# Cross attention in a one-core encoder layer: two heads' values in one 512-column projection, the attention's small products put at stated steps of the projections, and the last two heads' products moved later

## The chip, the cores and the metric

The kernel runs on one core of a Trainium2 chip. The metric is device time in microseconds (us), the median of several runs; lower is better. The profile shows one execution of the same program.

## The reference

One encoder layer (256 tokens, width 2048, float32) has four sub-layers: a feed-forward block, a pair of gated token mixers, a cross attention to 256 memory tokens, and a second feed-forward block. Each reads a normalized x and adds a normalized output to x. The change is in the cross attention, where four heads of width 256 attend from 256 tokens to 256 memory tokens:

```python
D_MODEL, SEQ, N_MEM, MEM_HEADS, MEM_HEAD = 2048, 256, 256, 4, 256

def memory_xattn(h, mem, n_mem, w_cq, w_ckv, w_co):
    B, S, _ = h.shape
    M = mem.shape[1]
    q = (h @ w_cq).reshape(B, S, MEM_HEADS, MEM_HEAD)
    kv = (rmsnorm(mem, n_mem) @ w_ckv).reshape(B, M, MEM_HEADS, 2 * MEM_HEAD)
    k, v = kv[..., :MEM_HEAD], kv[..., MEM_HEAD:]
    s = jnp.einsum('bqhd,bmhd->bhqm', q, k).astype(jnp.float32) * (MEM_HEAD ** -0.5)
    p = jax.nn.softmax(s, axis=-1).astype(v.dtype)
    o = jnp.einsum('bhqm,bmhd->bqhd', p, v).reshape(B, S, MEM_HEADS * MEM_HEAD)
    return o @ w_co

# in the layer, after the mixers:
h = rmsnorm(x, n_x_pre[l])
x = x + rmsnorm(memory_xattn(h, mem, n_mem[l], w_cq[l], w_ckv[l], w_co[l]), n_x_post[l])
```

## The kernel before

**Projections.** A float32 weight matrix streams from HBM in tiles of 128 x 1024 numbers (`wraw`, four buffers, loaded by the SP queue). ACT writes the rounded part of a tile to `whi` (line 368) and DVE the remainder to `wlo` (line 369); both are rings of three slots, so the split of a tile waits until TensorE (PE) has done with the tile three before it. Activations are kept as two such parts too (`hT`, `mT`, `oT`). PE then makes three products where a plain one would make one.

There are two forms of a projection. `lin_ch` leaves the result with channels on partitions: the weights are stationary, and per step k (128 rows of the weight) and per 128 channels there is one product with both parts of the activations as 512 moving columns (line 424) and one of `wlo` with 256 columns (line 428). `lin_tok` leaves tokens on partitions: the activations are stationary, the weights move, and per step k and per 128 tokens t there are three products as wide as the projection's column block (lines 463, 464, 465). Both are generators that yield at steps: `lin_ch` once per k, `lin_tok` once per (k, t). The result is in PSUM: `psm` (tag `mm`, four banks) for projections, `pst` (tag `tr`, two) and `pss` (tag `sm`, two) for small products.

**The cross attention** (`xattn`). `kv(h)` makes one head's keys (`lin_ch`, 256 columns, tile `kT`) and values (`lin_tok`, 256 columns, tile `xv`, copied out of PSUM by ACT at line 1829). `query(h)` is a `lin_ch` of 256 columns. `attend(h, q)` makes, for each half t of the tokens, the scores (line 1854, tile `xsc`), their softmax (maximum on DVE, lines 986 and 987; exponential on ACT, line 989; division on DVE, lines 990 and 991; tile `p`), and the two 128 x 128 transposes of `p` (line 1859, tile `xpt`), which ACT copies to `pT` (line 1860); then the values' products (line 1865, tile `xo`) and their split into `oT` (line 656, ACT and DVE). Scores and values are plain float32, which PE takes in two passes each.

**What sets the order.** The keys and values of heads 0 and 1 come first, then those of head 2 beside the normalization of x (`pre_norm`: 32 transposes of x, tile `tr`, line 691, split into `hT` at lines 658 and 659), then the queries and the heads, then head 3's keys and values, then the output projection `w_co` (`lin_tok`, four blocks of 512 columns) with head 3's attention inside its first block. Where the program says nothing, a list scheduler orders each engine's instructions by priority (the order in which they are written) and by its own estimate of when operands are ready; on each engine the resulting order is fixed, and an engine waits at an instruction whose operands are late. Inside `tc.manual_schedule(engines={PE})` PE's instructions keep the order in which they are written. The weights of `w_ckv` are laid out on the host in blocks (`_CUTS`), one block after another in the order of the loads.

Of the kernel before, what the change touches and what calls it, by code (L numbers as in the profile page):

```python
# [10 lines left out]
F32 = mybir.dt.float32  # L11
F32R = mybir.dt.float32r
I32 = mybir.dt.int32
AF = mybir.ActivationFunctionType
# [4 lines left out]
P = 128  # L19
D = 2048  # L20
T = 256
NT = T // P
KD = D // P
# [205 lines left out]
class Layer:  # L229
# [396 lines left out]
    def row(self, r):  # L626

        nc = self.nc
        ps = self.pss.tile([P, T], F32, tag="sm", name="rB")
        for t in range(NT):  # L630
            nc.tensor.matmul(
                ps[:, t * P : (t + 1) * P], r[t].broadcast_to([P, P]), self.ident, start=True, stop=True)
# [1180 lines left out]
    def xattn(self, m, xsp):  # L1813
        nc, a, tc = self.nc, self.a, self.tc
        with tc.tile_pool(name="xat", bufs=1) as pool:
            squares = pool.tile([P, 2, 8, T], F32, tag="oT", name="squares")
            squares = [squares[:, i] for i in range(2)]
            mem, feed = self.pre_norm_input(a["memT"], "n_mem", pool, squares)
            mr, mrow = self.square_stats(squares)
            todo = [lambda k=k: feed(k, 4) for k in range(0, KD, 4)] + [mr, int, mrow]  # L1820
            update = self.mix_out(*m, xsp, lambda: todo and todo.pop(0)())
            kT = pool.tile([P, 8, T], F32, name="kT")
            v = pool.tile([P, NT, 1024], F32, name="xv")

            def kv(h):
                self.lin_ch(a["w_ckv"], KD, h * 512, 256, mem,
                            lambda j, ps: nc.vector.tensor_mul(kT[:, 2 * h + j, :], ps, mrow()))
                self.lin_tok(a["w_ckv"], KD, h * 512 + 256, 256, mem[:, :, 0], mem[:, :, 1],
                             lambda t, ps: nc.scalar.activation(
                                 out=v[:, t, h * 256 : (h + 1) * 256], in_=ps, func=AF.Copy, scale=mr()[t]))  # L1830
# [12 lines left out]
            def query(h):  # L1843
                q = pool.tile([P, 2, T], F32, tag="q", name="q", bufs=4)
                self.lin_ch(a["w_cq"], KD, h * 256, 256, hq,
                            lambda j, ps: nc.vector.tensor_mul(q[:, j, :], ps, row()))
                return q

            def attend(h, q):
                pT = pool.tile([P, 2, T], F32, tag="pT", name="pT", bufs=2)  # L1850
                for t in range(NT):
                    ps = self.pss.tile([P, T], F32, tag="sm", name="xsc")
                    for j in range(2):
                        nc.tensor.matmul(  # L1854
                            ps, q[:, j, t * P : (t + 1) * P], kT[:, 2 * h + j, :], start=(j == 0), stop=(j == 1))
                    p = self.softmax(pool, ps, 1.0 / 16)
                    pt = self.pst.tile([P, 2, P], F32, tag="tr", name="xpt")
                    for j in range(2):
                        nc.tensor.transpose(pt[:, j, :], p[:, j * P : (j + 1) * P], self.ident)
                    nc.scalar.copy(out=pT[:, :, t * P : (t + 1) * P], in_=pt)  # L1860
                for j in range(2):
                    po = self.pss.tile([P, T], F32, tag="sm", name="xo")
                    for m in range(NT):
                        vs = slice(h * 256 + j * P, h * 256 + (j + 1) * P)
                        nc.tensor.matmul(po, v[:, m, vs], pT[:, m, :], start=(m == 0), stop=(m == NT - 1))  # L1865
# [10 lines left out]
            return self.post_norm(  # L1876
                lambda c, ev, passage: self.lin_tok(
                    a["w_co"], 8, c * 512, 512, o[:, 0], o[:, 1], ev, 8 * (c == 3), passage),
                a["n_x_post"], False, "n_ffn2_pre", None, xsp)

    def store(self, update):
        for t in range(NT):
# [7 lines left out]
def layer(ctx: ExitStack, tc, a):  # L1890
# [21 lines left out]
_MOVING = {"w_ukv": lambda i, m: False, "w_ckv": lambda i, m: i % 2 == 1}  # L1912
_ROWS = ("n_ffn1_post", "n_mix_post", "n_x_post", "n_ffn2_post", "b_gate", "lnx_w", "lnx_b")


def _tiles(w, cuts, moving):

    nk, out, c0 = w.shape[0] // P, [], 0
    if isinstance(cuts, int):
        cuts = [cuts] * (w.shape[1] // cuts) + [w.shape[1] % cuts] * (w.shape[1] % cuts > 0)  # L1920
    for i, n in enumerate(cuts):
        kt = WT // n
        order = np.arange(n).reshape(-1, 2).T.reshape(-1) if moving(i, n) else np.arange(n)
        for k in range(0, nk, kt):
            out.append(w[k * P : (k + kt) * P, c0 + order].reshape(-1, P, n).transpose(1, 0, 2).reshape(-1))
        c0 += n
    assert c0 == w.shape[1]
    return np.concatenate(out)


def _wide_tiles(w):

    out, order = [], np.arange(512).reshape(-1, 2).T.reshape(-1)
    ks = [k for item in _wide_order() for k in (item if isinstance(item, tuple) else (item,))]
    for c0 in range(0, D, WT):
        for k in ks:
            out.append(w[k * P : (k + 1) * P, c0 + np.concatenate([order, 512 + order])].reshape(-1))
        for h in range(2):
            for k in range(WIDE, KF, 2):
                x = w[k * P : (k + 2) * P, c0 + h * 512 + order]  # L1940
                out.append(x.reshape(-1, P, 512).transpose(1, 0, 2).reshape(-1))
    return np.concatenate(out)


def _layout(inputs):
    f = lambda n: np.ascontiguousarray(np.asarray(inputs[n]))
    arr = {"x": f("x")[0], "mem": f("mem")[0], "positions": f("positions")[0].reshape(NT, P).T}
    for n in ("x", "mem"):
        arr[n + "T"] = arr[n].T.reshape(KD, P, T).transpose(1, 0, 2)
    for n in _WEIGHTS:  # L1950
        arr[n] = f(n)[0]
    for n in _ROWS:
        arr[n] = f(n)[0].reshape(1, -1)
    mu = f("mu_shift")[0]
# [36 lines left out]
```

## Time and profile before

| | |
|---|---|
| time, median of 3 runs | 2170.76 us (2169.75 to 2171.69) |
| time of the profiled execution | 2169.75 us, its span 2167.9 us |
| granted TensorE clock | 0.999 |
| PE, busy share of the span | 99% |
| PE's weight loads | 89% |
| DVE | 75% |
| ACT | 55% |
| POOL | 5% |
| loads of `w_ckv` | 32 of 512 KB, on the SP queue |

The cross attention takes the profile's stretch from 1299.81 us, where the first keys begin, to about 1466 us, in the first block of `w_co`. A matmul's own record overlaps the next one's; what a matmul costs PE is the distance from its start to the next start, and the text below uses such distances. A record of PE can stand for two passes or be missing, so counts are taken from the code.

### The profile page before, as it was taken

The numbers are of one execution on the slowest core, as the hardware profiler recorded it, in microseconds if no ns is written. First come the engines' busy times: TensorE is split into PE (matmuls) and PEld (weight loads), VectorE is DVE, ScalarE is ACT, GpSimd is POOL, SyncE is SP. The second block draws the span as 40 slices with busy tenths as digits, with TensorE's granted clock in tenths as the row PEclk, the third lists the DMA queues.
The fourth block names the chain that finished last, engine by engine and source line by source line (L and its number), as shares of the span: only waits on it lengthen the run. The fifth ranks groups of instructions, "written<-read, shape, count | busy, mean of one in ns | idle before, by whom it ended". The sixth has DMA issues, their size and how long they took to land.

```text
span 2167.9 us, 35391 instructions
## 1 busy us (share of the span) xinstructions
PE 2151.0 (99%) x13568; PEld 1925.1 (89%) x13568; DVE 1634.2 (75%) x2437; ACT 1195.6 (55%) x1811; POOL 107.4 (5%) x184
## 2 busy tenths in 40 slices
PE   9999999999999999999999999999999999999998
PEld 8999999988888999988878889988999999998887
DVE  7777766679898678777778866657777766669797
ACT  7555555555556665664444646446555555555463
POOL 0000000000000100101342000000000000000000
PEclk9999999999999999999999999999999999999999
DMA  7666666666667664555868766547666666666665
GB/s 251 201 201 203 200 201 202 200 228 206 224 234 235 224 227 144 184 175 182 250 200 263 289 208 194 175 160 227 198 202 203 199 202 202 200 217 226 215 223 194
DMA packets 132361, 453.51 MB, mean 209 GB/s; under 512 B 16352, under 2 KB 17888, under 8 KB 131936
## 3 DMA queue, kind: packets, MB, share of 16 engines
q1 hardware_dynamic: 123408, 429.84, 60.9%
q0 software_dynamic: 7920, 20.98, 3.1%
q8 instruction: 106, 1.74, 0.3%
q10 hardware_dynamic: 864, 0.44, 0.1%
q14 instruction: 63, 0.52, 0.1%
HBM read 438.61 MB, written 12.59 MB: 208 GB/s over the span
## 4 chain that ended last, share of the span: by engine, by line
PE 50%; DVE 3%; issue 1%; DMA 0%; ACT 0%; DVEq 0%; POOLq 0%; ACTq 0%
PE mm L424 16%; PE mm L428 8%; PE mm L463 5%; PE mm L464 5%; PE mm L465 5%; PE mm L552 3%; PE mm L551 3%; PE mm L550 3%; DVE wlo L369 1%; DVE tm L1444 0%; DVE TT L1447 0%; PE xo L1865 0%; PE xsc L1854 0%; PE tr L668 0%; DMA LT<-ld 0%
## 5 line engine op out<-in xcount | busy, mean ns | idle before, releaser
L424 PE MATMUL mm<-hT,whi 128*128 128x512 f32 x3280 | 1077.0, 383 | 2.1 <-DVE hT L659 1.1
L369 DVE TENSOR_TENSOR wlo<-wraw,whi 128x1024 fp32r<-128x1024 f32 (+3 forms) x653 | 783.8, 1202 | 381.7 <-ACT whi L368 372.2
L368 ACT CAST whi<-wraw 128x1024 fp32r<-128x1024 f32 (+3 forms) x653 | 672.6, 1031 | 542.4 <-PE mm L465 174.8
L428 PE MATMUL mm<-hT,wlo 128*128 128x256 f32 x3280 | 878.5, 273 | 0.6 <-DVE wlo L369 0.6
L424 PEld LDWEIGHTS mm<-hT,whi 128*128 128x128 f32 x3280 | 613.4, 189 | 83.5 <-ACT whi L368 3.3
L428 PEld LDWEIGHTS mm<-hT,wlo 128*128 128x128 f32 x3280 | 628.9, 192 | 7.2 <-DVE wlo L369 1.6
L463 PE MATMUL mm<-whi,hT 128*128 128x512 f32 (+2 forms) x512 | 183.1, 358 | 0.0
L464 PE MATMUL mm<-wlo,hT 128*128 128x512 f32 (+2 forms) x512 | 179.5, 351 | 1.2 <-DVE wlo L369 0.9
L465 PE MATMUL mm<-whi,hT 128*128 128x512 f32 (+2 forms) x512 | 178.7, 349 | 0.9 <-DVE hT L659 0.9
L436 ACT COPY half<-mm 128x256 f32<-128x256 f32 x206 | 75.6, 368 | 114.3 <-PE mm L424 114.3
L550 PE MATMUL mm<-whi,mh 128*128 128x512 f32 x320 | 121.3, 379 | 0.0
L551 PE MATMUL mm<-wlo,mh 128*128 128x512 f32 x320 | 121.3, 379 | 0.0
L552 PE MATMUL mm<-whi,ml 128*128 128x512 f32 x320 | 121.3, 379 | 0.0
L437 DVE TENSOR_TENSOR half<-half,mm 128x256 f32<-128x256 f32 x206 | 85.9, 418 | 39.3 <-ACT half L436 39.1
L464 PEld LDWEIGHTS mm<-wlo,hT 128*128 128x128 f32 x512 | 97.1, 190 | 14.8 <-DVE wlo L369 5.5
L463 PEld LDWEIGHTS mm<-whi,hT 128*128 128x128 f32 x512 | 97.1, 190 | 11.5 <-issue 1.0
L465 PEld LDWEIGHTS mm<-whi,hT 128*128 128x128 f32 x512 | 97.1, 190 | 11.1 <-DVE hT L659 2.1
L540 ACT CAST room<-wraw 128x1024 fp32r<-128x1024 f32 (+1 forms) x68 | 60.3, 895 | 74.3 <-DVE wraw L577 71.7
L541 DVE TENSOR_TENSOR wlo<-wraw,whi 128x1024 fp32r<-128x1024 f32 x72 | 85.9, 1222 | 15.9 <-ACT whi L540 14.7
L540 ACT CAST whi<-wraw 128x1024 fp32r<-128x1024 f32 x72 | 73.0, 1046 | 28.8 <-PE mm L465 8.7
L541 DVE TENSOR_TENSOR room<-wraw,room 128x1024 fp32r<-128x1024 f32 (+1 forms) x68 | 69.6, 1029 | 0.0
L552 PEld LDWEIGHTS mm<-whi,ml 128*128 128x128 f32 x320 | 60.5, 189 | 8.6
(373 smaller groups left out, 2785.5 us busy)
## 6 DMA issues: line engine op xcount, KB each, us to landing
wraw<-in_w_ffn_up SPq DMA_DIRECT2D x171, 512.0 KB, 4.2
wraw<-in_w_ffn_gate SPq DMA_DIRECT2D x170, 512.0 KB, 4.2
wraw<-in_w_ffn_down SPq DMA_DIRECT2D x128, 512.0 KB, 4.9
wraw<-in_w_in SPq DMA_DIRECT2D x124, 512.0 KB, 4.1
raws<-in_w_ffn_down SPq DMA_DIRECT2D x40, 512.0 KB, 4.9
wraw<-in_w_o SPq DMA_DIRECT2D x32, 512.0 KB, 3.9
wraw<-in_w_ckv SPq DMA_DIRECT2D x32, 512.0 KB, 3.5
wraw<-in_w_oa SPq DMA_DIRECT2D x16, 512.0 KB, 3.5
```

What stands on the lines that cost most here:

```text
L368: cast = self.last_cast = nc.scalar.copy(out=hi[:, e], in_=raw[:, e])
L369: self.last_split = nc.vector.tensor_sub(out=lo[:, e], in0=raw[:, e], in1=hi[:, e].bitcast(F32))
L424: both = lambda: nc.tensor.matmul(ps[j], hi[:, s], self.woven(x[:, k]), start=(k == 0), stop=(k == nk - 1))
L428: nc.tensor.matmul(ps[j][:, 0, :], lo[:, s], self.woven(x[:, k, 0]), start=False, stop=False)
L463: nc.tensor.matmul(ps[t], part(xh, t, k), hi, start=(k == first and not begun), stop=False, **more)
L464: nc.tensor.matmul(ps[t], part(xh, t, k), lo, start=False, stop=False, **more)
L465: self.last_mm = nc.tensor.matmul(ps[t], part(xl, t, k), hi, start=False, stop=(k == last), **more)
L540: self.last_cast = nc.scalar.copy(out=hi, in_=raw)
L541: self.last_split = nc.vector.tensor_sub(out=lo, in0=raw, in1=hi.bitcast(F32))
L550: nc.tensor.matmul(bank, xh, hi, start=start, stop=False)
L551: nc.tensor.matmul(bank, xh, lo, start=False, stop=False)
L552: nc.tensor.matmul(bank, xl, hi, start=False, stop=stop)
```

## The change

The values of two heads are made by one `lin_tok` of 512 columns (`vals`), before the queries for heads 0 and 1, after them for heads 2 and 3; the keys of heads 2 and 3 are made beside the normalization. `w_ckv` is laid out on the host in the new order. `attend` is cut into `scores`, `turned` (all four transposes in one PSUM tile, one copy) and `values` (both halves in one PSUM tile, one split), and these are called at given steps of the projections, in whose PE order they stay: the scores of head h after some four or five steps of the next projection, the transposes six or seven steps later, the values in the projection after that. Scores of head 3 stand in the values of heads 2 and 3; the values' products of heads 2 and 3 stand in the first block of `w_co`.

```diff
-            def kv(h):
-                self.lin_ch(a["w_ckv"], KD, h * 512, 256, mem,
-                            lambda j, ps: nc.vector.tensor_mul(kT[:, 2 * h + j, :], ps, mrow()))
-                self.lin_tok(a["w_ckv"], KD, h * 512 + 256, 256, mem[:, :, 0], mem[:, :, 1],
-                             lambda t, ps: nc.scalar.activation(
-                                 out=v[:, t, h * 256 : (h + 1) * 256], in_=ps, func=AF.Copy, scale=mr()[t]))
-            for h in range(2):
-                kv(h)
+            def keys(h, c):
+                return self.lin_ch_steps(a["w_ckv"], KD, c * 256, 256, mem,
+                                         lambda j, ps: nc.vector.tensor_mul(kT[:, 2 * h + j, :], ps, mrow()))
+            def vals(h, c):
+                return self.lin_tok_steps(a["w_ckv"], KD, c * 256, 512, mem[:, :, 0], mem[:, :, 1],
+                                          lambda t, ps: nc.scalar.activation(
+                                              out=v[:, t, h * 256 : (h + 2) * 256], in_=ps, func=AF.Copy,
+                                              scale=mr()[t]))
...
+            def run(steps, at={}):
+                for i, _ in enumerate(steps):
+                    for f, h in at.get(i, ()):
+                        f(h)
+            for steps in (keys(0, 0), keys(1, 1), vals(0, 2)):
+                run(steps)
             base = tc.cur_priority
             with self.priority(base + 1000):
-                for h in range(2, 3):
-                    kv(h)
+                for steps in (keys(2, 4), keys(3, 5)):
+                    run(steps)
                 after = tc.cur_priority
             hq, _, row = self.pre_norm("n_x_pre", update)
...
+            def turned(h):
+                pt = self.pst.tile([P, 2, T], F32, tag="tr", name="xpt")
+                for t in range(NT):
                     for j in range(2):
-                        nc.tensor.transpose(pt[:, j, :], p[:, j * P : (j + 1) * P], self.ident)
-                    nc.scalar.copy(out=pT[:, :, t * P : (t + 1) * P], in_=pt)
+                        nc.tensor.transpose(
+                            pt[:, j, t * P : (t + 1) * P], p[h][t][:, j * P : (j + 1) * P], self.ident)
+                pT[h] = pool.tile([P, 2, T], F32, tag="pT", name="pT", bufs=2)
+                nc.scalar.copy(out=pT[h], in_=pt)
+            def values(h):
+                po = self.pst.tile([P, 2, T], F32, tag="tr", name="xo")
                 for j in range(2):
-                    po = self.pss.tile([P, T], F32, tag="sm", name="xo")
                     for m in range(NT):
                         vs = slice(h * 256 + j * P, h * 256 + (j + 1) * P)
-                        nc.tensor.matmul(po, v[:, m, vs], pT[:, m, :], start=(m == 0), stop=(m == NT - 1))
-                    self.split(po, o[:, 0, 2 * h + j, :], o[:, 1, 2 * h + j, :])
-            qs = [query(0), query(1)]
-            attend(0, qs[0])
-            qs.append(query(2))
-            attend(1, qs[1])
-            qs.append(query(3))
-            attend(2, qs[2])
-            kv(3)
-            attend(3, qs[3])
...
+                        nc.tensor.matmul(po[:, j, :], v[:, m, vs], pT[h][:, m, :], start=(m == 0), stop=(m == NT - 1))
+                s = slice(2 * h, 2 * h + 2)
+                self.split(po, o[:, 0, s, :], o[:, 1, s, :])
+            run(query(0))
+            with tc.manual_schedule(engines={mybir.EngineType.PE}):
+                run(query(1), {4: [(scores, 0)], 10: [(turned, 0)]})
+                run(query(2), {3: [(values, 0), (scores, 1)], 10: [(turned, 1)]})
+                run(query(3), {3: [(values, 1), (scores, 2)], 10: [(turned, 2)]})
+                run(vals(2, 6), {4: [(scores, 3)], 11: [(turned, 3)]})
+            def lin(c, ev, passage):
+                steps = self.lin_tok_steps(
+                    a["w_co"], 8, c * 512, 512, o[:, 0], o[:, 1], ev, 8 * (c == 3), passage)
+                if c == 0:
+                    with tc.manual_schedule(engines={mybir.EngineType.PE}):
+                        return run(steps, {2: [(values, 2), (values, 3)]})
+                run(steps)
...
-    "w_o": 512, "w_cq": 256, "w_ckv": 256, "w_co": 512, "w_ffn2_gate": 256, "w_ffn2_up": 256,
+    "w_o": 512, "w_cq": 256, "w_ckv": [256, 256, 512] * 2, "w_co": 512, "w_ffn2_gate": 256, "w_ffn2_up": 256,
```

On PE, in the projection beside which head 0's softmax runs, the transposes of `p` (tile `xpt`) stand in two pairs before:

```order
L424 MATMUL mm<-hT,whi 128x512
L1859 MATMUL xpt<-ident,p 128x128 x2
L428 MATMUL mm<-hT,wlo 128x256
L424 MATMUL mm<-hT,whi 128x512
L1859 MATMUL xpt<-ident,p 128x128 x2
L428 MATMUL mm<-hT,wlo 128x256
```

and in one piece of four in the changed kernel:

```order
L424 MATMUL mm<-hT,whi 128x512
L428 MATMUL mm<-hT,wlo 128x256
L1875 MATMUL xpt<-ident,p 128x128 x4
L424 MATMUL mm<-hT,whi 128x512
L428 MATMUL mm<-hT,wlo 128x256
```

Between the scores and the first transposes stand 15 projection products before, and 24 after; between the scores and the last transposes 17 before and 24 after.

On PE, at the end of the heads, head 3's scores (`xsc`) stand between its own values' projection and the first products of `w_co` (those that read `oT`) before:

```order
L464 MATMUL mm<-wlo,hT 128x256
L465 MATMUL mm<-whi,hT 128x256
L1854 MATMUL xsc<-kT,q 128x256 x4
L463 MATMUL mm<-whi,oT 128x512
L464 MATMUL mm<-wlo,oT 128x512
```

In the changed kernel the products of `pT` and `xv` of heads 2 and 3 (tile `xo`) stand nine products into `w_co`, and nothing but `w_co` follows:

```order
L463 MATMUL mm<-whi,oT 128x512
L464 MATMUL mm<-wlo,oT 128x512
L465 MATMUL mm<-whi,oT 128x512
L1885 MATMUL xo<-pT,xv 128x256 x8
L463 MATMUL mm<-whi,oT 128x512
```

On ACT, at the same place, the copies of the last values (`xv`) out of PSUM stand like this in the changed kernel; before, the two copies of 256 columns had the same split of a weight tile (`whi`) between them, and head 3's exponentials and `pT` behind them:

```order
L1878 COPY pT<-xpt 128x512
L368 CAST whi<-wraw 128x1024 x4
L1831 ACTIVATE xv<-mm,rstd 128x512
L368 CAST whi<-wraw 128x1024
L1831 ACTIVATE xv<-mm,rstd 128x512
L656 CAST oT<-xo 128x512 x2
```

Head 3's softmax and its copy `pT` moved ahead of these copies. SP's queue of loads is the same row for row.

More of the change, by code (lines that the diff above doesn't have):

```diff
@@ L1823, in xattn, with query @@
             v = pool.tile([P, NT, 1024], F32, name="xv")
-            def kv(h):
-                self.lin_ch(a["w_ckv"], KD, h * 512, 256, mem,
-                            lambda j, ps: nc.vector.tensor_mul(kT[:, 2 * h + j, :], ps, mrow()))
-                self.lin_tok(a["w_ckv"], KD, h * 512 + 256, 256, mem[:, :, 0], mem[:, :, 1],
-                             lambda t, ps: nc.scalar.activation(
-                                 out=v[:, t, h * 256 : (h + 1) * 256], in_=ps, func=AF.Copy, scale=mr()[t]))
-            for h in range(2):
-                kv(h)
+            def keys(h, c):
[6 more added lines that the diff above has]
+                                              scale=mr()[t]))
+            q = {}
+            def query(h):
+                q[h] = pool.tile([P, 2, T], F32, tag="q", name="q", bufs=4)
+                return self.lin_ch_steps(a["w_cq"], KD, h * 256, 256, hq,
+                                         lambda j, ps: nc.vector.tensor_mul(q[h][:, j, :], ps, row()))
+            def run(steps, at={}):
[4 more added lines that the diff above has]
+                run(steps)
             base = tc.cur_priority
             with self.priority(base + 1000):
-                for h in range(2, 3):
-                    kv(h)
+                for steps in (keys(2, 4), keys(3, 5)):
+                    run(steps)
                 after = tc.cur_priority
@@ L1841, in xattn, with scores @@
             o = pool.tile([P, 2, 8, T], F32R, tag="oT", name="oT")
[L1843 to L1850, printed above, removed]
+            p = {}
+            def scores(h):
+                p[h] = []
                 for t in range(NT):
@@ L1854, in attend @@
                         nc.tensor.matmul(
-                            ps, q[:, j, t * P : (t + 1) * P], kT[:, 2 * h + j, :], start=(j == 0), stop=(j == 1))
-                    p = self.softmax(pool, ps, 1.0 / 16)
-                    pt = self.pst.tile([P, 2, P], F32, tag="tr", name="xpt")
-                    for j in range(2):
-                        nc.tensor.transpose(pt[:, j, :], p[:, j * P : (j + 1) * P], self.ident)
-                    nc.scalar.copy(out=pT[:, :, t * P : (t + 1) * P], in_=pt)
+                            ps, q[h][:, j, t * P : (t + 1) * P], kT[:, 2 * h + j, :],
@@ new lines, in scores @@
+                            start=(j == 0), stop=(j == 1))
+                    p[h].append(self.softmax(pool, ps, 1.0 / 16))
+            pT = {}
+            def turned(h):
+                pt = self.pst.tile([P, 2, T], F32, tag="tr", name="xpt")
+                for t in range(NT):
+                    for j in range(2):
+                        nc.tensor.transpose(
+                            pt[:, j, t * P : (t + 1) * P], p[h][t][:, j * P : (j + 1) * P], self.ident)
+                pT[h] = pool.tile([P, 2, T], F32, tag="pT", name="pT", bufs=2)
+                nc.scalar.copy(out=pT[h], in_=pt)
@@ L1868, in xattn @@
-            qs = [query(0), query(1)]
-            attend(0, qs[0])
-            qs.append(query(2))
-            attend(1, qs[1])
-            qs.append(query(3))
-            attend(2, qs[2])
-            kv(3)
-            attend(3, qs[3])
[L1876 to L1879, printed above, removed]
+                        nc.tensor.matmul(po[:, j, :], v[:, m, vs], pT[h][:, m, :], start=(m == 0), stop=(m == NT - 1))
@@ L1881, in store @@
+            def lin(c, ev, passage):
[5 more added lines that the diff above has]
+                run(steps)
+            return self.post_norm(lin, a["n_x_post"], False, "n_ffn2_pre", None, xsp)
     def store(self, update):
@@ L1909 @@
     "w_in": [512, 320] + [256] * 8 + [512] * 2 + [256] + [512] * 8,
-    "w_o": 512, "w_cq": 256, "w_ckv": 256, "w_co": 512, "w_ffn2_gate": 256, "w_ffn2_up": 256,
+    "w_o": 512, "w_cq": 256, "w_ckv": [256, 256, 512] * 2, "w_co": 512, "w_ffn2_gate": 256, "w_ffn2_up": 256,
 }
-_MOVING = {"w_ukv": lambda i, m: False, "w_ckv": lambda i, m: i % 2 == 1}
+_MOVING = {"w_ukv": lambda i, m: False}
 _ROWS = ("n_ffn1_post", "n_mix_post", "n_x_post", "n_ffn2_post", "b_gate", "lnx_w", "lnx_b")
@@ L1953, in _layout @@
         arr[n] = f(n)[0].reshape(1, -1)
+    kv = np.arange(2048).reshape(4, 2, 256)
+    kv = [c for h in (0, 2) for c in (kv[h, 0], kv[h + 1, 0], kv[h, 1], kv[h + 1, 1])]
+    arr["w_ckv"] = arr["w_ckv"][:, np.concatenate(kv)]
     mu = f("mu_shift")[0]
```

## Prediction

> **What bounds the kernel now.** I read the page's head first, then the waits of TensorE (PE) over the cross attention, then PE's timeline row by row.
>
> ```profile
> span 2167.9 us, 35391 instructions
> PE 2151.0 (99%) x13568; PEld 1925.1 (89%) x13568; DVE 1634.2 (75%) x2437; ACT 1195.6 (55%) x1811; POOL 107.4 (5%) x184
> ```
>
> PE is busy 99% of the span. Its waits between 1299.8 and 1466.2 us are one line:
>
> ```profile
> PE tr L691 <- DVE hT L659: 0.3, 1, 0.3
> ```
>
> So in this stage the end is set by PE's own stream, and a gain has to be a shorter stream: products that cost less, or stops too short to be listed as waits. Both are read from starts. First the projections (start, duration, engine, line):
>
> ```profile
> 1310.29 0.27 PE L463 MATMUL mm<-whi,hT 128*128 128x256 f32 x1
> ...
> 1321.00 0.38 PE L424 MATMUL mm<-hT,whi 128*128 128x512 f32 x1
> ...
> 1331.49 0.27 PE L463 MATMUL mm<-whi,hT 128*128 128x256 f32 x1
> ...
> 1452.16 0.38 PE L465 MATMUL mm<-whi,oT 128*128 128x512 f32 x1
> ...
> 1465.76 0.38 PE L465 MATMUL mm<-whi,oT 128*128 128x512 f32 x1
> ```
>
> One head's values are 16 steps x 2 token halves x 3 = 96 products of 256 columns: 10.71 us, 111.6 ns each. One head's keys (or a query) are 64 products: 10.49 us, 0.328 a pair. In `w_co` the last two rows are 63 products of 512 columns apart: 13.60 us, 215.9 ns each. A wide product costs 7.3 ns less than two narrow ones.
>
> Then the small products. Head 0's scores, and its transposes:
>
> ```profile
> 1388.87 0.38 PE L424 MATMUL mm<-hT,whi 128*128 128x512 f32 x1
> 1389.09 1.89 PE L1854 MATMUL xsc<-kT,q 128*128 128x256 f32 x8
> 1390.63 0.57 PE L424 MATMUL mm<-hT,whi 128*128 128x512 f32 x1
> 1391.04 0.27 PE L428 MATMUL mm<-hT,wlo 128*128 128x256 f32 x1
> ...
> 1393.11 0.38 PE L424 MATMUL mm<-hT,whi 128*128 128x512 f32 x1
> 1393.35 0.44 PE L1859 MATMUL xpt<-ident,p 128*128 128x128 f32 x2
> 1393.55 0.36 PE L428 MATMUL mm<-hT,wlo 128*128 128x256 f32 x1
> 1393.74 0.38 PE L424 MATMUL mm<-hT,whi 128*128 128x512 f32 x1
> 1394.20 0.44 PE L1859 MATMUL xpt<-ident,p 128*128 128x128 f32 x2
> 1394.39 0.36 PE L428 MATMUL mm<-hT,wlo 128*128 128x256 f32 x1
> 1394.59 0.38 PE L424 MATMUL mm<-hT,whi 128*128 128x512 f32 x1
> ```
>
> From 1388.87 to 1391.04 is 2.17 us; two wide products are 0.43, so the eight score passes cost 1.73. From 1393.11 to 1394.59 is 1.48; the two pairs in it are 0.66, so four transposes cost 0.82. The row at 1393.74 is where it shows: its successor starts 0.46 later, not 0.22.
>
> **What undisturbed transposes cost** is seen in the normalization of x:
>
> ```profile
> 1342.20 1.04 PE L691 MATMUL tr<-ident,X 128*128 128x128 f32 x8
> 1343.00 0.46 PE L424 MATMUL mm<-hT,whi 128*128 128x512 f32 x1
> 1343.30 0.27 PE L428 MATMUL mm<-hT,wlo 128*128 128x256 f32 x1
> ...
> 1346.02 0.38 PE L424 MATMUL mm<-hT,whi 128*128 128x512 f32 x1
> 1346.67 1.06 PE L691 MATMUL tr<-ident,X 128*128 128x128 f32 x8 [0.27 <-DVE hT L659]
> ...
> 1367.68 0.38 PE L424 MATMUL mm<-hT,whi 128*128 128x512 f32 x1
> ```
>
> Eight without a wait take 1.10 us less the 0.22 of the product behind them: 0.88, or 0.11 each. Four are 0.44, and head 0 paid 0.82.
>
> **The change, part by part.**
>
> *Values 512 wide.* 192 narrow products for two heads become 96 wide ones: 96 x 7.3 ns = 0.70 us, twice: -1.40 us. The ends: -1.4 by these rows, 0 if the excess of the narrow ones stays for a reason that isn't their width. I take -1.40, since the wide row is from the same form of projection. The Trainium skill ("TensorE: Matmul & The Clock Gate", Back-to-back issue gap) gives a warm product N / 2.4 + 2.5 ns, which would be 215.8 and 109.2 ns. The trace agrees on the wide one (215.9) and has the narrow one at 111.6; by the rule the term would be -0.48 us.
>
> *Transposes in one piece, later.* Three heads first, from a row of the stage table (stretch, length, then busy times):
>
> ```profile
> 1389.09:1433.48 44.39, 44.09 (x253) 39.07 (x252) 26.81 (x54) 21.61 (x43) 0.00 (x0) 1.00 0.43 142
> ...
> 1447.66 0.38 PE L465 MATMUL mm<-whi,oT 128*128 128x512 f32 x1
> ...
> 1449.27 0.38 PE L463 MATMUL mm<-whi,oT 128*128 128x512 f32 x1
> ...
> L1865 PE MATMUL xo<-pT,xv 128*128 128x256 f32 x32 | 7.6, 381 | 0.0
> L1854 PE MATMUL xsc<-kT,q 128*128 128x256 f32 x32 | 7.6, 379 | 0.0
> ```
>
> The stretch holds three 64-product units (31.47) and the scores and values of heads 0 to 2, six bursts of 1.73 (10.38; the two groups are alike): 2.54 us are left for twelve transposes. Head 3's stand between the two rows of `w_co`: 1.61 less four wide products (0.86) is 0.75. Together 3.29 us for 16. In one piece of four after the softmax is done they are 0.44 and a restart. Head 0's first pair (1393.35 to 1393.74, less the 0.11 of the product in it) took 0.28 where two are 0.22, so a restart is 0 to 0.06; I take 0.02, since the piece of eight had none: 4 x 0.46 = 1.84. So -1.45 us, if the softmax is over by then. Ends: -1.5 (no restart) and 0 (each still waits as long).
>
> Is it over? Head 0's scores begin at 1389.09; the last division of `p` ends at 1394.14:
>
> ```profile
> 1393.79 0.35 DVE L991 TENSOR_SCALAR p<-p,sm 128x256 f32<-128x256 f32 x1
> ...
> L656 DVE TENSOR_TENSOR mT<-tr,mT 128x512 fp32r<-128x512 f32 x8 | 5.1, 681 | 0.0
> ```
>
> That is 5.05 us. In the new order the transposes come 1.73 + 12 pairs x 0.328 = 5.66 us after the scores' start for head 0, and 14 pairs or 21 wide products (6.3 us) for the others: 0.6 us and 1.2 us to spare. On DVE the maxima of heads 1 and 2 now stand behind the `oT` remainder of the head before, 512 wide: 0.68 by the like row above. So their last division may come 0.7 later than the 5.05, and is still ahead.
>
> *Scores and values moved and joined.* The passes are as many as before, and eight passes cost 1.73 whether alone or behind others: 0. What the move needs is `q`. Head 0's scores now come ten pairs after the row broadcast `rB`, at 1378.17 + 0.44 + 3.28 = 1381.89 in the old clock; the second half of `q` was done at 1381.80:
>
> ```profile
> 1378.17 0.61 PE L631 MATMUL rB<-ident,rstd 128*128 128x128 f32 x4
> ...
> 1381.37 0.43 DVE L1846 TENSOR_TENSOR q<-half,row 128x256 f32<-128x256 f32 x1
> ```
>
> The margin is 0.09: +0.05, ends 0 and +0.4. The other heads have a 1.73 us burst of values ahead, so 0.
>
> *The last values' copies.* `values` of heads 2 and 3 stand nine wide products, 1.94 us, behind the last one of `vals`. ACT copies both halves out first, with one weight split between them:
>
> ```profile
> 1444.07 0.47 ACT L1829 ACTIVATE xv<-mm,rstd 128x256 f32<-128x256 f32 x1 [1.30 <-PE mm L465]
> 1444.44 1.03 ACT L368 CAST whi<-wraw 128x1024 fp32r<-128x1024 f32 x1
> ...
> 1444.20 1.89 PE L1854 MATMUL xsc<-kT,q 128*128 128x256 f32 x8
> ...
> L1246 ACT ACTIVATE vc<-mm,rstd 128x512 f32<-128x512 f32 x4 | 2.7, 684 | 1.9 <-PE mm L465 1.9
> ```
>
> The stream's end was 1444.20; the split began 0.24 behind it, and 0.95 later the second copy. That copy, now 0.68 (the like form), ends 0.24 + 0.95 + 0.68 = 1.87 after the end: 0.07 before it is needed. 0, ends 0 and +0.5. The split into `oT` has five (k, t) steps of `w_co` (15 x 0.216 = 3.2 us) before its first use: covered.
>
> *The normalization beside the keys.* Both fillers are 21 us; the new one is two key units. Here the scheduler cuts 32 transposes into one piece of eight and six of four. From 1342.20 to 1367.68 is 25.48; less 10.49 and 10.71 they cost 4.28 now, 0.76 over 32 x 0.11. A piece of four waits for one PSUM tile, not two, but there are more restarts: 0, with ends -0.76 and +1.1.
>
> *At nothing:* the copies of `pT` and `oT` in one go are ACT and DVE work under PE's stream (covered while PE waits for neither); the loads of `w_ckv` keep size, number and place in SP's queue, and the host's layout is outside the time.
>
> Sum: -1.40 - 1.45 + 0.05 = **-2.8 us**. The span of 2167.9 becomes 2165.1, the profiled execution's 2169.75 becomes 2166.95. The median of the runs shown is 1.0 above that execution, so I predict 2170.76 - 2.8 = **2168.0 us**.
>
> **Rivals.**
>
> 1. *The waits move along.* PE's order is now fixed, so a late softmax stops it. If the last division comes 1.0 us later than now for head 0, and 1.6 for the others, each head pays 0.36 again, all that was to be saved there: only the values' 1.40 are left, 2169.4 us. For it: the 0.6 us to spare of head 0. Against it: the 1.2 of the others.
> 2. *The narrow products' excess isn't their width* and stays: only the transposes gain, -1.40, 2169.4 us too. For it: beside a wide product, in the pairs of keys and queries, a narrow one takes 0.328 - 0.216 = 0.112 as well, so the excess could come with the change of stationary operand. Against it: the wide products of `w_co` change theirs as often and take 0.216. The Trainium skill's rule above would lie between, at 2168.9.
> 3. *Slower: the fixed order stops PE longer than now.* The place is the transposes of all four heads. It ends above 2170.76 when their waits add up to 2.8 us (0.7 a head, so a softmax of 6.4 us for head 0 and 7.0 for the others, against 5.05), and is a measurable loss at 7.1 us. At 1.0 a head it gives 2172.0. For it: nothing but the written order now says when the transposes come. Against it: in DVE's new order no weight split stands between a head's first maximum and its last division; in the 5.05 there was one.
> 4. *More than summed:* the normalization's stops vanish too (-0.76): -3.6, which is 2167.2, and 2166.2 in a set of runs whose median lies as low as the lowest of those shown.
>
> **How the numbers follow.** A difference under 0.2% (4.3 us) is about what a measurement of this kernel cannot tell from none. Chances: my sum 0.57; rival 1, 0.17; rival 2, 0.08; rival 3, 0.08 (0.03 of it beyond 0.2%); rival 4, 0.10. A gain over 4.3 needs 0.6 beyond every term's good end, which the runs' spread of 1.9 us can just give: 0.07 of rival 4. So faster 0.07, same 0.90, slower 0.03. The range goes from rival 4's low end, 2166.1, to rivals 1 and 2 with the normalization's +1.1, 2170.6; it leaves out rival 3 and the edge of rival 4. My own sum's range is 2167.0 to 2169.2.
>
> **What would show it.** Values: 96 products of about 216 ns in 20.7 us, twice. Transposes of `p`: pieces of four with 0.44 to 0.5 us between the neighbouring products' starts. No new line for `q`, `p` or `xv` among PE's waits. From the first keys to the end of `w_co`'s first block about 2.8 us less, and every later stage the same length. I am wrong if PE's weight loads wait for DVE's `p` or ACT's `xv` by more than 0.5 us a head, if the wide values take 21.4 us, or if a stage outside the cross attention changes by over 1 us.

## The result and the profile after

The changed kernel takes 2167.23 us (median of 22 runs, 2165.92 to 2169.11), the kernel before 2170.78 us (22 runs on the same chip, 2168.61 to 2172.96): a ratio of 0.9984, 95% interval 0.9978 to 0.9990, or 3.6 us less, between 2.2 and 4.8. That is under the 0.2% which the prediction took as its bound, and inside its range; it said 2168.0.

The head of the page after, for the changed kernel:

```profile
span 2165.5 us, 34992 instructions
PE 2149.8 (99%) x13376; PEld 1921.2 (89%) x13376; DVE 1634.6 (75%) x2433; ACT 1194.0 (55%) x1799; POOL 107.4 (5%) x184
```

PE is still busy 99% of the span, so it is still its own bound. The 192 products fewer are what is left when 384 narrow ones become 192 wide ones. The profiled execution took 2167.24 us, 0.01 above the median.

PE's waits from the first keys to the passage (the transposes of x that lead from `w_co` into the feed-forward block, line 168), for the changed kernel:

```profile
PE tr L168 <- DVE X L770: 0.4, 1, 0.4
PE tr L691 <- DVE hT L659: 0.2, 1, 0.2
```

No line for `p`, `q` or `xv`: the fixed order waits for none of the softmaxes. The second line is the normalization's, as before; the first is new. Now the rows of PE behind the terms of the sum (start, duration, operation), again of the changed kernel:

```profile
1320.85 0.38 PE L463 MATMUL mm<-whi,hT 128*128 128x512 f32 x1
...
1341.57 1.04 PE L691 MATMUL tr<-ident,X 128*128 128x128 f32 x8
...
1381.20 1.89 PE L1864 MATMUL xsc<-kT,q 128*128 128x256 f32 x8
1382.74 0.57 PE L424 MATMUL mm<-hT,whi 128*128 128x512 f32 x1
...
1386.75 0.27 PE L428 MATMUL mm<-hT,wlo 128*128 128x256 f32 x1
1386.86 0.60 PE L1875 MATMUL xpt<-ident,p 128*128 128x128 f32 x4
1387.21 0.46 PE L424 MATMUL mm<-hT,whi 128*128 128x512 f32 x1
1387.51 0.27 PE L428 MATMUL mm<-hT,wlo 128*128 128x256 f32 x1
```

The two heads' values run from 1320.85 to 1341.57: 20.72 us for 96 products, 215.8 ns each. The piece of four transposes takes 0.35 us to the next start, and the product behind it 0.30 instead of 0.22: 0.44 in all, exactly four times 0.11. The same rows stand at heads 1 to 3, so 16 transposes cost 1.75 us.

Both kernels' stage can be cut at the same three instants. First the kernel before, then the changed one: the first keys, the last product ahead of the passage, and the passage's first transposes.

```profile
1299.81 0.38 PE L424 MATMUL mm<-hT,whi 128*128 128x512 f32 x1
...
1487.12 0.38 PE L465 MATMUL mm<-whi,oT 128*128 128x512 f32 x1
1487.51 0.63 PE L168 MATMUL tr<-ident,X 128*128 128x128 f32 x4
```

```profile
1299.89 0.38 PE L424 MATMUL mm<-hT,whi 128*128 128x512 f32 x1
...
1484.28 0.38 PE L465 MATMUL mm<-whi,oT 128*128 128x512 f32 x1
1485.09 0.63 PE L168 MATMUL tr<-ident,X 128*128 128x128 f32 x4 [0.42 <-DVE X L770]
```

The stage is 187.70 us before and 185.20 after, 2.50 less. But the product ahead of the passage holds PE for 0.81 us after and 0.39 before: 0.42 us come back there, for a late X. Without it the gain would be 2.92. Whether those 0.42 us belong to the change is the first question below.

### The profile page after: what moved, and what is told of

Its sections match the earlier page's. It is cut to its first block, busy times and chain, and to the rows that moved or that the text cites. A ratio compares the mean times of both kernels' runs of the same rounds, so it can differ in the third digit from the quotient of the medians.

```text
span 2165.5 us, 34992 instructions
## 1 busy us (share of the span) xinstructions
PE 2149.8 (99%) x13376; PEld 1921.2 (89%) x13376; DVE 1634.6 (75%) x2433; ACT 1194.0 (55%) x1799; POOL 107.4 (5%) x184
## 4 chain that ended last, share of the span: by engine, by line
PE 49%; DVE 3%; DMA 1%; issue 1%; ACT 0%; POOL 0%; DVEq 0%; POOLq 0%; ACTq 0%
PE mm L424 16%; PE mm L428 8%; PE mm L463 5%; PE mm L464 5%; PE mm L465 5%; PE mm L550 3%; PE mm L552 3%; PE mm L551 3%; DVE wlo L369 1%; DMA wraw<-in_w_ffn_gate 0%; DVE tm L1444 0%; DVE TT L1447 0%; PE xo L1885 0%; PE xsc L1864 0%; DMA ab<-vsh 0%
## 5 line engine op out<-in xcount | busy, mean ns | idle before, releaser
L463 PE MATMUL mm<-whi,hT 128*128 128x512 f32 (+1 forms) x448 | 172.4, 385 | 0.0
L464 PE MATMUL mm<-wlo,hT 128*128 128x512 f32 (+1 forms) x448 | 168.5, 376 | 1.5 <-DVE wlo L369 1.2
L465 PE MATMUL mm<-whi,hT 128*128 128x512 f32 (+1 forms) x448 | 167.7, 374 | 0.9 <-DVE hT L659 0.9
L464 PEld LDWEIGHTS mm<-wlo,hT 128*128 128x128 f32 x448 | 84.7, 189 | 16.6 <-DVE wlo L369 5.7
L463 PEld LDWEIGHTS mm<-whi,hT 128*128 128x128 f32 x448 | 84.6, 189 | 13.2 <-issue 1.0
L465 PEld LDWEIGHTS mm<-whi,hT 128*128 128x128 f32 x448 | 84.7, 189 | 12.8 <-DVE hT L659 2.1
L551 PEld LDWEIGHTS mm<-wlo,mh 128*128 128x128 f32 x320 | 60.5, 189 | 8.6
```

The costliest lines, as they stand in the source:

```text
L463: nc.tensor.matmul(ps[t], part(xh, t, k), hi, start=(k == first and not begun), stop=False, **more)
L464: nc.tensor.matmul(ps[t], part(xh, t, k), lo, start=False, stop=False, **more)
L465: self.last_mm = nc.tensor.matmul(ps[t], part(xl, t, k), hi, start=False, stop=(k == last), **more)
L551: nc.tensor.matmul(bank, xh, lo, start=False, stop=False)
```

## The experiments

The theory: PE's stream is the bound; it became 1.4 us shorter by wider products and 1.5 us by transposes that no longer wait for the softmax, and all else in the change costs next to nothing. The rivals: the narrow products' excess isn't their width; the transposes gained by being made in one piece, or by a softmax that ends earlier, not by standing later; something is given back at the end of the stage.

The medians of single kernels are known to about 1 us, so each verdict rests on distances between starts of PE in the trace, which repeat to 0.03 us wherever no engine or load is late. The segments are: from the first keys to the normalization's first transposes (A), to head 0's first scores (B), to the first product that reads `oT` (C), to the passage's first transposes (D), and their sum. B and C hold different work before and after, and are compared only among kernels of one kind.

| kernel | A | B | C | D | sum | median, us | ratio to before (95%) |
|---|---|---|---|---|---|---|---|
| before | 42.39 | 46.89 | 56.65 | 41.77 | 187.70 | 2170.78 | |
| before, again | 42.40 | 46.88 | 56.65 | 41.76 | 187.69 | 2171.52 | 1.0001 (0.9993 to 1.0010) |
| before, values of heads 0 and 1 wide | 41.68 | 47.17 | 56.65 | 41.77 | 187.27 | 2170.08 | 0.9999 (0.9990 to 1.0008) |
| changed | 41.68 | 39.63 | 61.00 | 42.89 | 185.20 | 2167.23 | 0.9984 (0.9978 to 0.9990) |
| changed, again | 41.69 | 39.62 | 61.00 | 42.53 | 184.84 | 2167.06 | 0.9985 (0.9976 to 0.9994) |
| values in narrow products | 42.37 | 39.63 | 61.68 | 42.48 | 186.16 | 2168.96 | 0.9992 (0.9984 to 1.0001) |
| transposes early | 41.68 | 39.62 | 64.25 | 42.48 | 188.03 | 2170.61 | 0.9997 (0.9988 to 1.0006) |
| transposes late, in halves | 41.68 | 39.62 | 61.00 | 42.48 | 184.78 | 2167.20 | 0.9986 (0.9977 to 0.9994) |
| transposes just behind the softmax | 41.68 | 39.63 | 60.99 | 42.48 | 184.78 | 2167.61 | 0.9987 (0.9978 to 0.9995) |
| thin covers taken away | 41.68 | 38.97 | 61.95 | 42.73 | 185.33 | 2167.87 | 0.9985 (0.9976 to 0.9994) |
| normalization stated | 41.68 | 39.13 | 61.00 | 42.56 | 184.37 | 2167.05 | 0.9981 (0.9973 to 0.9990) |
| normalization stated, second placing | 41.68 | 38.65 | 61.00 | 42.47 | 183.80 | 2166.41 | 0.9980 (0.9971 to 0.9989) |

### Both kernels once more

No edit. The changed kernel:

> The changed kernel once more, to see what of its profile belongs to the change. Its gain in the stage was 1.40 (wide values) and 1.54 us (transposes), of which the profile shows 0.42 us given back at the first transposes of the passage behind w_co (a stop of 0.8 us before them, where the kernel before has 0.39). Theory A: that stop is set by when the weight loads land in one execution; the second profile then has another size of it (between 0 and 1 us more than the kernel before) while the wide values (20.72 us) and the pieces of four (0.44 us each) stay the same to 0.02 us. Theory B: the change causes it, since PE now comes 2.9 us earlier to loads that do not come earlier; then the stop is 0.8 us again. Time by both: 2167.2 us, 3.6 below the kernel before.

The kernel before:

> The kernel before once more, to see which parts of its profile repeat. Theory: from the start of the first keys to the passage's first transposes it takes 187.7 us again (to 0.1), with the same stops at the transposes of p; what differs between executions lies ahead of the first keys (they began between 1299.8 and 1302.7 us in six profiles of these kernels). Rival: the stage itself varies by a microsecond, so that the 2.86 us between the two kernels in it are partly chance. Time by both: 2170.7 us.

The end of `w_co` in the second profile of the changed kernel:

```profile
1485.05 0.38 PE L465 MATMUL mm<-whi,oT 128*128 128x512 f32 x1
1485.50 0.63 PE L168 MATMUL tr<-ident,X 128*128 128x128 f32 x4
```

The stop is now 0.45 us (0.39 before), no wait is listed, and A, B and C repeat to 0.01. In six of the other kernels with the changed end, D is 42.47 or 42.48 once their own stops are taken off. So theory A holds for the size: the 0.42 us are one execution's. In that execution ACT's last weight splits stood behind late loads:

```profile
1475.95 1.05 ACT L368 CAST whi<-wraw 128x1024 fp32r<-128x1024 f32 x1 [2.49 <-DMA wraw<-in_w_co]
1480.25 1.04 ACT L368 CAST whi<-wraw 128x1024 fp32r<-128x1024 f32 x1 [2.67 <-DMA wraw<-in_w_ffn_gate]
```

Behind them DVE's part of the split and the update of X came late. (The second profile has like waits, 2.46 and 2.34 us, and stops 0.06: the place is near its edge.) That it is near its edge may well be the change's: three of the nine profiles with the changed end stop there (0.42, 0.06 and 0.09 us), none of the three with the old end; no run settles it. The kernel before repeats to 0.01 us in the whole stage. The change's gain there is 187.70 less 184.84: 2.86 us, or 2.92 where no load is late.

### The values in narrow products

```diff
-            nc.tensor.matmul(ps[t], part(xh, t, k), lo, start=False, stop=False, **more)
...
+            def product(x, w, start, stop):
+                if start or stop or not getattr(self, "narrow", False):
+                    return nc.tensor.matmul(ps[t], x, w, start=start, stop=stop, **more)
+                for i in range(2):
+                    nc.tensor.matmul(
+                        ps[t][:, i * 256 : (i + 1) * 256], x, w[:, i * 128 : (i + 1) * 128, :],
+                        start=False, stop=False, **more)
...
+            product(part(xh, t, k), lo, False, False)
```

(and so for the other two products; `narrow` is set in `vals` alone, and the first and last product of a sum stay wide)

> The changed kernel with 92 of the 96 products of each two-head value projection issued as two of 256 columns, same stationary operand, same loads, order and tiles. Theory (width costs): 7.3 ns more for each pair, 92 x 7.3 = 0.67 us a projection, 1.34 us in all: each projection takes 21.4 instead of 20.72 us, and the median is 2168.6. Rival (the excess of the narrow products of the kernel before came with something else than width): 20.72 us again and 2167.2. By the Trainium skill's rule of N / 2.4 + 2.5 ns a product the pair would cost 2.6 ns more, 0.48 us in all, 2167.7.

A is 0.69 us longer and C 0.68: 1.37 us for 184 pairs, 7.4 ns a pair. Rows of the first projection of this kernel, where a row marked x2 is two narrow products:

```profile
1321.79 0.38 PE L465 MATMUL mm<-whi,hT 128*128 128x512 f32 x1
1322.01 0.38 PE L467 MATMUL mm<-wlo,hT 128*128 128x256 f32 x2
1322.23 0.39 PE L467 MATMUL mm<-whi,hT 128*128 128x256 f32 x2
1322.45 0.38 PE L465 MATMUL mm<-whi,hT 128*128 128x512 f32 x1
```

So the excess comes with the narrow products: it is there though loads, layout and order are the wide kernel's, and though both halves have the same stationary operand. Rival 2 of the prediction falls. One thing stays open: each half loads that operand anew (PE's weight loads go from 13376 to 13560 in this kernel), so the run does not tell the narrow width from the load that comes with every product. The change takes both away. The Trainium skill's rule ("TensorE: Matmul & The Clock Gate", Back-to-back issue gap: N / 2.4 + 2.5 ns, given there for a single product on its own) would make it 2.5 ns a pair; the trace agrees with it at 512 columns (215.8) and not at 256 (111.6 measured, 109.2 by the rule).

### The transposes early, and late in halves

Early, the changed kernel's steps:

```diff
-                run(query(1), {4: [(scores, 0)], 10: [(turned, 0)]})
+                run(query(1), {4: [(scores, 0)], 6: [(turned, 0)]})
```

(heads 1 and 2 at step 5, head 3 at step 6)

> The changed kernel with the transposes of p four or five steps earlier: 3.0 us after the scores' start, where the softmax ends 4.12 (head 0), 3.73 (heads 1 and 2) and about 4.1 us (head 3) after it. DVE's and ACT's orders are the same. Theory (PE's order is fixed, so it stops until p is there; two of the four transposes can be made before): 0.9 + 0.5 + 0.5 + 0.9 us and about 0.1 us of restart each, 3.2 us in all, listed as waits for DVE's p; 2170.4 us, the whole gain gone. Rival (the gain at the transposes came from making four in one go, not from their distance): 2167.2 as with the late ones, no listed wait.

Late, but in two pieces of two (for heads 0 to 2 at steps 9 and 10, for head 3 at 10 and 11):

```diff
-                run(query(1), {4: [(scores, 0)], 10: [(turned, 0)]})
+                run(query(1), {4: [(scores, 0)], 9: [(first, 0)], 10: [(second, 0)]})
```

> The changed kernel with the transposes of each head in two pieces of two, one step apart (the second where the piece of four stood, the first one step before), each with its own PSUM tile and copy: late as in the changed kernel, cut as in the kernel before. Theory (distance, not grouping, was what the kernel before paid): a pair costs 0.22 us and a restart of 0.02 to 0.06, so 16 transposes take 1.9 to 2.2 us instead of 1.75: at most +0.5 us, 2167.2 to 2167.7. Rival (grouping): the pairs cost 0.41 us each as in the kernel before, 3.29 in all: +1.5 us, 2168.8.

The early one's waits of PE for the softmax, and its first piece with the division of `p` for which it waits:

```profile
PE xpt L1875 <- DVE sm L990: 1.0, 3, 0.7
PE xpt L1875 <- DVE p L991: 0.5, 1, 0.5
```

```profile
1384.64 0.27 PE L428 MATMUL mm<-hT,wlo 128*128 128x256 f32 x1
1385.43 0.90 PE L1875 MATMUL xpt<-ident,p 128*128 128x128 f32 x4 [0.51 <-DVE p L991]
1386.08 0.46 PE L424 MATMUL mm<-hT,whi 128*128 128x512 f32 x1
```

```profile
1385.02 0.35 DVE L991 TENSOR_SCALAR p<-p,sm 128x256 f32<-128x256 f32 x1
...
1385.48 0.35 DVE L991 TENSOR_SCALAR p<-p,sm 128x256 f32<-128x256 f32 x1
```

C is 3.25 us longer (3.2 expected) and the median is the kernel before's, within its interval. The waits listed add up to 1.5 us only: the rest is stops within the piece, between its second and third transpose, and the slower restart. One piece of four is no help when it stands too early.

In halves and late, C is 61.00 us, the same as with one piece. Its first pair, and the second one step later:

```profile
1388.97 0.38 PE L1876 MATMUL xpt<-ident,p 128*128 128x128 f32 x2
1389.10 0.46 PE L424 MATMUL mm<-hT,whi 128*128 128x512 f32 x1
1389.40 0.27 PE L428 MATMUL mm<-hT,wlo 128*128 128x256 f32 x1
...
1389.84 0.38 PE L1876 MATMUL xpt<-ident,p 128*128 128x128 f32 x2
1389.98 0.46 PE L424 MATMUL mm<-hT,whi 128*128 128x512 f32 x1
```

A pair costs 0.13 + (0.30 - 0.22) = 0.21 us, half of a piece of four. So the grouping was none of the 1.5 us. What was paid before was PE's stop for a softmax that was not over.

### The transposes just behind the softmax

Head 0's and head 3's transposes at step 8, those of heads 1 and 2 at step 7.

> The changed kernel with the transposes of p two or three steps earlier than there, 4.35 us after the scores' start, just behind the softmax (its last division ends 4.12, 3.73, 3.73 and 4.22 us after that start). Theory (a cover is worth nothing beyond the instant at which it suffices): no stop, the pieces of four cost 0.44 us each as in the changed kernel, 61.00 us from the first scores to the first product that reads oT, 2167.2. Rival (a division that ends 0.1 to 0.6 us ahead is not yet visible to PE, or the earlier copy of pT comes between the weight splits on ACT): up to 0.3 us a head, 2168.4.

Head 0's scores and PE's first piece, and DVE's last division, in this kernel:

```profile
1383.59 1.89 PE L1864 MATMUL xsc<-kT,q 128*128 128x256 f32 x8
...
1387.93 0.60 PE L1875 MATMUL xpt<-ident,p 128*128 128x128 f32 x4
1388.29 0.46 PE L424 MATMUL mm<-hT,whi 128*128 128x512 f32 x1
```

```profile
1387.35 0.35 DVE L991 TENSOR_SCALAR p<-p,sm 128x256 f32<-128x256 f32 x1
```

The division ends at 1387.70, 0.23 us before the piece, and nothing stops: C is 60.99. The 1.5 us that the changed kernel leaves between them buy nothing.

Set beside the kernel before, this run says more. For heads 0 to 2 the piece stands 16 projection products behind the scores, where the two pairs stood 15 and 17 products behind them for head 0: this is about the old place (4.35 us after the scores' start, against 4.26 and 5.11 before). What differs is the softmax. Before, its last division ended 5.05 us after the scores' start for heads 0 to 2; now it ends 4.12 us (head 0) and 3.73 us (heads 1 and 2) after it. DVE's maxima of head 0, in the kernel before with a weight split between them, and in the changed kernel:

```profile
1390.17 0.42 DVE L986 TENSOR_REDUCE mx<-xsc 128x1 f32<-128x256 f32 x1
1390.50 1.21 DVE L369 TENSOR_TENSOR wlo<-wraw,whi 128x1024 fp32r<-128x1024 f32 x1
...
1392.03 0.41 DVE L986 TENSOR_REDUCE mx<-xsc 128x1 f32<-128x256 f32 x1
```

```profile
1382.86 0.75 DVE L986 TENSOR_REDUCE mx<-xsc 128x1 f32<-128x256 f32 x2
```

So for heads 0 to 2, which carry 1.2 of the 1.5 us, DVE's new order is enough: the transposes need not have moved. (Head 3's softmax became only 0.2 us shorter, 4.39 to 4.23.) Whether the later place would have been enough by itself no run shows; against the old end of the softmax it has 0.6 us to spare for head 0 and 1.3 for heads 1 and 2.

### The thin covers taken away

```diff
-                run(query(1), {4: [(scores, 0)], 10: [(turned, 0)]})
+                run(query(1), {3: [(scores, 0)], 10: [(turned, 0)]})
...
-                        return run(steps, {2: [(values, 2), (values, 3)]})
+                        return run(steps, {1: [(values, 2), (values, 3)]})
```

> The changed kernel with the two thin covers taken away: head 0's scores one step (0.66 us) earlier, the values' products of heads 2 and 3 one step (0.65 us) earlier in w_co. In the changed kernel's profile the second half of q is ready 0.08 us before head 0's scores begin, the second copy of xv 0.11 us before those products begin. Theory A (PE needs the late half at once, as the prediction counted): it stops 0.58 and 0.54 us: +1.1 us, 2168.3. Theory B (the first two passes of 0.216 us read only the early half, so that the covers are 0.43 us thicker than counted): 0.15 and 0.11 us and a restart each: +0.3 us, 2167.5.

PE at both places, with DVE's second half of `q` between them:

```profile
1381.48 2.18 PE L1864 MATMUL xsc<-kT,q 128*128 128x256 f32 x8
1383.32 0.57 PE L424 MATMUL mm<-hT,whi 128*128 128x512 f32 x1
...
1444.72 3.88 PE L1885 MATMUL xo<-pT,xv 128*128 128x256 f32 x16
1448.25 0.57 PE L463 MATMUL mm<-whi,oT 128*128 128x512 f32 x1
```

```profile
1381.62 0.42 DVE L1840 TENSOR_TENSOR q<-half,row 128x256 f32<-128x256 f32 x1
```

The eight score passes now reach the next product after 1.84 us instead of 1.54 (1381.20 to 1382.74 in the changed kernel): 0.29 us more by the unrounded starts. The sixteen passes of `xo` take 3.53 against 3.26: 0.26 more. Together 0.55, between theory B's 0.3 and theory A's 1.1. B's mechanism is the right one: in the trace the first two passes run, 0.43 us, and the third begins 0.06 us after `q` is done at 1382.04. What B left out is that the pass which restarts takes 0.32 us instead of 0.22; that tenth stands at both places. So a short stop costs 0.1 us beyond its wait.

### The wide values of two heads alone

```diff
-            for h in range(2):
-                kv(h)
+            keys(0, 0)
+            keys(1, 1)
+            vals(0, 2, 2)
```

(`vals(h, c, n)`: n heads' values in one projection; the rest of the kernel before as it was, `w_ckv` laid out to match)

> The kernel before with one part of the change alone: the values of heads 0 and 1 as one projection of 512 columns (their keys ahead of it, the weights laid out to match); heads 2 and 3, the scores, transposes and values' products as before. Theory: 96 x 7.3 ns = 0.70 us less up to the normalization's first transposes (42.39 becomes 41.68 us), and since its order there then reads as in the changed kernel (one piece of eight and six of four), 0.19 us more in it: -0.5 us, 2170.2. The transposes of p cost 3.29 us as before. Rival (the normalization's 0.19 us came with the two key projections beside it, which this kernel doesn't have there): -0.70 us, 2170.0, and 4.28 us there.

A is 41.68, 0.71 us less, to the hundredth what the changed kernel has. B is 0.28 longer than before, so the theory's sign holds at the normalization, with half as much again as expected: its transposes get the cut order of the changed kernel without the second projection of keys beside them. So the new making of the first two heads' keys and values is enough for that. C is 56.65, as before: the transposes of `p` cost what they did. The sum is 0.43 us less; the time alone (0.9990 to 1.0008) could not tell that from nothing.

### The normalization's transposes at stated places

```diff
+            if between is not None:
+                between(c)
...
+            with tc.manual_schedule(engines={mybir.EngineType.PE}):
+                hq, _, row = self.pre_norm("n_x_pre", update, between)
```

(`between(c)` writes the next 8, 8 and 7 steps of the keys of heads 2 and 3 behind each piece of eight transposes, and the rest behind the fourth; a step is two pairs of products. In the second placing it is 9, 8 and 7.)

> The changed kernel with the normalization's transposes at stated places too: four pieces of eight, with 16, 16 and 14 key pairs between them, in a PE order that is fixed. Theory (its 4.47 us are 3.5 us of transposes and the rest stops of a cut order): four pieces of 0.88 us, with up to 0.04 of restart each, 3.5 to 3.7 us; -0.8 to -1.0 us against the changed kernel, 2166.2. Rival (the splits of hT on DVE and ACT are the limit; each piece needs both PSUM tiles back, and four splits of 0.44 us and a weight split of 1.23 us stand between): PE stops before the pieces by as much or more, 2167.2 or later.

> The kernel with the normalization's transposes at stated places, with 18 instead of 16 key pairs between its first and second piece. In the earlier placing one piece still stopped 0.44 us for the last split of hT of the piece before (DVE, 0.52 us after the piece began), and the stage was 0.47 us shorter than the changed kernel's. Theory (distance is all that is missing): the second piece, 0.66 us later, does not stop; the stage from the first keys to the passage takes 183.9 us (184.84 in the changed kernel), 2166.2 in all. Rival (one of the later pieces, or the query's first products, now waits for splits that moved behind one more weight split on DVE): 184.4 us or more, 2167.0.

The second piece of the first placing, and the four pieces of the second:

```profile
1348.93 0.38 PE L691 MATMUL tr<-ident,X 128*128 128x128 f32 x2
1349.59 0.84 PE L691 MATMUL tr<-ident,X 128*128 128x128 f32 x6 [0.28 <-DVE hT L659]
1350.19 0.46 PE L424 MATMUL mm<-hT,whi 128*128 128x512 f32 x1
```

```profile
1345.63 1.04 PE L691 MATMUL tr<-ident,X 128*128 128x128 f32 x8
...
1352.39 1.04 PE L691 MATMUL tr<-ident,X 128*128 128x128 f32 x8
...
1358.51 1.04 PE L691 MATMUL tr<-ident,X 128*128 128x128 f32 x8
...
1363.97 1.04 PE L691 MATMUL tr<-ident,X 128*128 128x128 f32 x8
1364.76 0.46 PE L424 MATMUL mm<-hT,whi 128*128 128x512 f32 x1
```

The first placing gained about half of what was expected (B 39.13 against 39.62): one piece still stopped within itself, for the fourth split of `hT` of the piece before. Two pairs more ahead of it, and none stops: B is 38.65, 0.97 us less than in the changed kernel, and the stage 183.80, 1.04 less. PE then has no wait at all listed in it. This version is the shortest stage of all, and with 2166.41 us it lies below both kernels, though only the trace, not the median, tells it from the changed one.

## The prediction, point by point

- *Values, -1.40.* Right. A fell by 0.71 (0.70 expected), and the narrow kernel prices a pair at 7.4 ns where 7.3 was taken; for 192 pairs that is 1.43.
- *Transposes of `p`, -1.45.* The price of a piece behind a finished softmax was right, 0.1 too dear: 3.29 became 1.75, so -1.54. The mis-sized part is the restart of 0.02 a piece: there is none where nothing stops. The 0.08 that the first product behind a piece takes longer is made up by the piece's own last transpose, which is 0.03 long.
- *Is the softmax over?* Yes, but not for the reason given alone. The prediction kept the old 5.05 us, or 0.7 more, and counted on the later place; the softmax itself became 0.9 to 1.3 us shorter for heads 0 to 2, and the run just behind it shows that this alone ends their stops. The prediction had seen the sign of it (no weight split between maximum and division, under rival 3) and put it into no term; the error was on the safe side. The fear that the maxima stand behind a wider remainder of `oT` came to nothing: 3.73 us for heads 1 and 2. Rivals 1 and 3 were described rightly (the early kernel is both of them, at +3.25 us), but their condition was 1.5 us away for head 0, not 0.6.
- *`q` and the last copies, +0.05 and 0.* Measured 0 and 0. The margins, 0.08 and 0.11 in the trace, are as counted; what was missed is that the first 0.43 us of passes don't read the late half, so that the covers were five to six times as thick.
- *Normalization, 0.* It cost +0.18: the 32 transposes and their stops take 4.46 us where they took 4.28. This step chose "more restarts against easier tiles: 0"; the cut order has three more pieces, and one stops longer. Rival 4's idea that the stops could vanish is true, but not of this change: it needs the places to be stated, and is then worth 0.97.
- *Every later stage the same length.* From the start of the passage's first transposes to the start of PE's last matmul it is 672.02 to 672.05 us in every profile. Just ahead of the passage, 0.42 us came back in one execution, which the prediction did not have; the second has 0.06.
- *The sum, -2.8.* The trace has -2.86, by the second profile. The parts named here make -2.80 of it: -0.71 and about -0.71 for the values, -1.54, +0.18, -0.08 for a restart that head 3's values had before, and +0.06 at the passage. That the sum is met so closely is in part luck: the normalization's +0.18 nearly cancels what the transposes, `q` and head 3's values brought beyond their terms. The median fell by 3.55 and, in the second set of runs, by 3.67. The 0.7 us between lie inside the interval (2.2 to 4.8), and no profile shows a place for them: ahead of the first keys PE's order is as before, and there the profiles differ by more than that (the first keys begin at 1299.8 us at the earliest and at 1303.9 at the latest). That part stays open.

## What to carry to other kernels

Where PE is busy 99%, read a gain from the distances between its starts, not from its list of waits: 1.5 us of waiting for a softmax stood in no line of that list, and they went once the softmax was over before PE came to the transposes, whether in one piece or in halves. State the place by the measured end of the chain that feeds it: 0.2 us behind it is enough, more buys nothing, and 0.7 to 1.2 us ahead of it costs 3.25 us, more than the whole change gains. Look at the chain as well as at the place: here the shorter softmax was enough for three heads of four. When wide products replace narrow ones, look also at the work that a scheduler places next to them; the normalization's transposes lost 0.2 to 0.3 us that way, and stating their places won back 1.0.

## What was unexpected of the hardware

- A stop inside a burst of float32 passes costs the wait, 0.05 to 0.06 us from the releasing instruction's end to the next pass, and one pass of 0.32 instead of 0.22 us: 0.1 us beyond the wait, at both places of the kernel without thin covers.
- Between the first keys and the passage, executions agree to 0.03 us in each segment where no load is late. The spread among the runs of one kernel, 4.4 us for the kernel before and 3.2 for the changed one, comes from elsewhere: the profiles place up to 4 us of it ahead of the first keys, and up to 0.4 us at the passage, where loads of 512 KB land 3.3 to 8.5 us after their issue.
